# Two-layer streaming encoder: order of work at the entrance of the seven-product feed-forward stage

## The chip, the core and the metric

The kernel runs on one core of a Trainium2 chip. The metric is the device time of one execution in microseconds (us), lower is better. The core's engines run side by side, each through its own queue in order: TensorE (PE in the profile, its weight loads PEld), VectorE (DVE), ScalarE (ACT), GpSimd (POOL), and SyncE (SP), which issues most of the DMA transfers. An engine that waits for a semaphore holds up everything behind it in its own queue.

## The reference, cut to what matters

Two layers. Each projects its input into three mixers, concatenates their outputs, and then does this (`finish` and `conv_ffn` of the reference):

```
x = layer_norm(ALPHA * x + mix @ w_out, ln1_g, ln1_b)
hg = x @ w_gate
hu = x @ w_up
conv = conv_b + sum(conv_w[j] * ext[:, j:j + t] for j in range(3))   # ext: hg with two rows ahead
f = (gelu(conv) * hu) @ w_down
x = layer_norm(ALPHA * x + f, ln2_g, ln2_b)
```

Everything is float32. There are 1024 prompt rows and 128 sample rows, so nine row tiles of 128; D_MODEL is 1024 and D_FF 2816 (22 chunks of 128).

## The kernel before, in words

**Products.** Each float32 operand is split into a high and a low float32r part; a product is three matmuls, high by high, high by low, low by high (`mm3`, L176 to L178). The split is a cast on ScalarE and a subtraction on VectorE. The gate and up projections of one chunk f are not four block products but seven, by a scheme in the manner of Strassen and Winograd: the products A11 by B11, A12 by B21, S2 by T2, S1 by T1, S4 by B22, S3 by T3 and A22 by T4. The A and S operands come from the weights (S1 to S4 are sums of blocks of the chunk's weights), the B and T operands from the normed rows (T1 to T4 are sums of their transposed blocks). The B and T operands are made once a layer; the weight operands anew for each chunk.

**The passage.** It lies between the output projection (`w_out`, product tiles pwo) and the loop over the 22 chunks (product tiles pg), once in each layer: at about 636 to 700 us of the span in layer 0 and 2068 to 2132 us in layer 1. Row tiles 0 to 4 (G1) are already turned into operands ahead of it. Row tiles 5 to 8 (G2, x_5 to x_8 in the rows) go through it one by one. `norm1` calls `norm_rows` on a tile: statistics on VectorE (BN_STATS, BN_AGGR), the small steps to scale and bias (bnsc: plus EPS on VectorE, L211; power of minus one half on GpSimd, L212; minus mean times scale on VectorE, L231), and the norm's application to 128x1024 on ScalarE (L232). Then `pair(j)` follows: eight transposes of the tile on TensorE (L1236), four 512-wide products that bring back B11 and B21 of the partner tile (L1276), eight affine steps on ScalarE (L1290), then on VectorE the sums T1 (L1292), T3 (L1295), T2 (L1296) and T4 (L1298), each split by `put` (L1226, L1227) into the operands: arb holds T1, ara B22, art T2, ar T3 and T4. Pairs 5, 6, 7 and 8 follow each other; pairs 5 to 7 stand among the last `w_out` units and pair 8 after the first two products of chunk 0 (A11 and A12). Then come A11 and A12 of chunk 1 (`early`), then the loop.

**Buffers.** The sum T1 of a pair lies in tail, one buffer for all pairs; tail also holds the weight sum S1. The other sums of a pair lie in temp or in the tile of the pair before. The four product buffers (pg, two PSUM banks each) also serve the transposes of pair 8.

**Weights.** `wnext` makes the next weight operand in a fixed list: A11 and A12 of chunks 0 and 1, then S2, S1, S4, S3 and A22 of chunk 0, and so on. At S2 it makes the sums on GpSimd (L1358 to L1360), at S4 one more (L1362); the split is a cast on ScalarE (L1364) and a subtraction on VectorE (L1365) into one of eight ring slots. Raw weights come by SyncE DMAs into two raw buffers (L1341); a load waits until the last reader of its buffer is through.

**Order.** The program is written in one order, and the build's scheduler then places the instructions on each engine as it thinks best; on an engine they then run strictly in that placed order. `tc.issue_after(i)` keeps what is written under it behind instruction i in the placed order. In the kernel before, T3 and T4 of all four pairs are written after pair 8 (the list `rests`), but the scheduler has put most of them right behind the sums that they split.

## Time and profile before

| what | value |
|---|---|
| median of 3 runs | 2881.7 us (2879.95 to 2882.68) |
| profiled execution, its own time | 2882.72 us |
| its span, first to last instruction | 2880.9 us |
| TensorE busy | 2793.0 us, 97% of the span |
| VectorE, ScalarE, GpSimd busy | 72%, 48%, 31% of the span |
| mean granted TensorE clock | 0.988 of full |

A row of a timeline has start, duration, engine, line, operation, output and inputs, and in brackets how long the engine stood idle before it and what ended that wait. Start-to-start distance is what an instruction costs its engine when the next one waits for nothing; the durations overlap a little. The waits view sums such idle times. The clock column is the granted TensorE clock as a share of 2.4 GHz; 0.5 would be 1.2 GHz throughout. Durations come from the one profiled execution.

### The profile page before, as it was taken

Reading aid. Unit: us, or ns where it says so; the run is one execution under the profiler, and the core shown is the slowest. Engines: PE = TensorE matmul, PEld = TensorE weight load, DVE = VectorE, ACT = ScalarE, POOL = GpSimd, SP = SyncE. Lnnn points to the kernel's source line nnn. Section 1 sums busy time; section 2 is a strip of 40 time slices with the busy share of each in tenths; the row PEclk is TensorE's granted clock in tenths of the full one; section 3 lists DMA queues with packets and bytes.
Section 4 is the critical chain, followed back from the end, with each engine's and each line's share of the span. In section 5 each row is a group of like instructions: output and inputs, shape, how many; then the busy total and the mean of one; then the engine's idle time right before and its main releaser. Section 6 shows DMA issues by size and latency. Waiting matters only on the chain. (4 is left out here: it accounts for less than half of the span.)

```text
span 2880.9 us, 51251 instructions
## 1 busy us (share of the span) xinstructions
PE 2793.0 (97%) x19444; PEld 2613.9 (91%) x19444; DVE 2061.6 (72%) x4580; ACT 1387.3 (48%) x2937; POOL 886.3 (31%) x891
## 2 busy tenths in 40 slices
PE   8999999998999999999999999989989999999998
PEld 8898898998999999888898988989889999997886
DVE  6899878768666666556678997787686666665656
ACT  5687656645333333421256885565553333334211
POOL 2334543443322232000433445334432223220003
PEclk9999999999999999999999999999999999999999
DMA  4121123132212222443212111231322121224421
GB/s 138 53 66 50 43 62 102 58 125 92 72 70 76 76 79 96 158 131 127 79 47 81 39 50 47 56 111 47 121 94 77 69 85 70 72 100 155 153 84 66
DMA packets 105013, 243.15 MB, mean 84 GB/s; under 512 B 21671, under 2 KB 42047, under 8 KB 104767
## 3 DMA queue, kind: packets, MB, share of 16 engines
q1 hardware_dynamic: 88014, 198.59, 21.3%
q10 hardware_dynamic: 16752, 41.29, 3.7%
q8 instruction: 153, 2.51, 0.3%
q14 instruction: 94, 0.76, 0.1%
HBM read 185.20 MB, written 54.64 MB: 83 GB/s over the span
## 5 line engine op out<-in xcount | busy, mean ns | idle before, releaser
L176 PE MATMUL pg<-ar,ring 128*128 128x288 f32 x1408 | 417.1, 296 | 10.1 <-ACT s L1449 4.2
L178 PE MATMUL pg<-ar,ring 128*128 128x288 f32 x1408 | 417.2, 296 | 0.0
L177 PE MATMUL pg<-ar,ring 128*128 128x288 f32 x1408 | 416.5, 296 | 0.0
L1364 ACT CAST ring<-raw 128x512 fp32r<-128x512 f32 x264 | 163.3, 622 | 422.8 <-PE pg L177 401.6
L128 POOL TENSOR_TENSOR ring<-raw,ring 128x512 fp32r<-128x512 f32 (+1 forms) x140 | 191.7, 1396 | 317.9 <-ACT ring L127 270.1
L571 ACT ACTIVATE spare<-sc,cand 128x896 bf16<-128x896 f32 (+5 forms) x262 | 244.7, 934 | 67.3 <-DVE cand L598 21.2
L176 PEld LDWEIGHTS pg<-ar,ring 128*128 128x128 f32 x1408 | 266.1, 189 | 11.7 <-ACT s L1449 4.6
L1365 DVE TENSOR_TENSOR ring<-raw,ring 128x512 fp32r<-128x512 f32 x264 | 203.7, 776 | 90.9 <-ACT ring L1364 90.9
L177 PEld LDWEIGHTS pg<-ar,ring 128*128 128x128 f32 x1408 | 266.2, 189 | 0.0
L178 PEld LDWEIGHTS pg<-ar,ring 128*128 128x128 f32 x1408 | 266.0, 189 | 0.0
L1540 DVE TENSOR_TENSOR s<-s,pg 128x576 f32<-128x576 f32 x220 | 164.4, 749 | 50.8 <-PE pg L178 48.3
L1650 DVE TENSOR_TENSOR acc<-acc,pdn 128x512 f32<-128x512 f32 x180 | 121.3, 683 | 89.3 <-PE pdn L178 88.7
L1484 DVE TENSOR_TENSOR hx<-s,pg 128x512 f32<-128x512 f32 x88 | 60.5, 688 | 150.5 <-PE pg L178 150.5
L176 PE MATMUL pwo<-ring,ar 128*128 128x256 f32 x576 | 166.9, 290 | 0.0
L177 PE MATMUL pwo<-ring,ar 128*128 128x256 f32 x576 | 163.8, 284 | 0.0
L178 PE MATMUL pwo<-ring,ar 128*128 128x256 f32 x576 | 163.8, 284 | 0.0
L565 DVE TENSOR_SCALAR_CACHE_REDUCE spare<-sc,cand 128x384 bf16<-128x384 f32 (+4 forms) x208 | 158.5, 762 | 1.9
L176 PE MATMUL pdn<-ring,ar 128*128 128x512 f32 x360 | 140.1, 389 | 0.0
L177 PE MATMUL pdn<-ring,ar 128*128 128x512 f32 x360 | 140.1, 389 | 0.0
L178 PE MATMUL pdn<-ring,ar 128*128 128x512 f32 x360 | 140.1, 389 | 0.0
L1489 ACT ACTIVATE ct<-hx,cwt 128x512 f32<-128x512 f32 x88 | 71.8, 816 | 127.7 <-DVE hx L1484 127.7
L176 PE MATMUL pvg<-ring,ar 128*128 128x256 f32 x432 | 127.8, 296 | 1.4 <-DVE sg L740 1.4
(427 smaller groups left out, 9434.7 us busy)
## 6 DMA issues: line engine op xcount, KB each, us to landing
raw<-w_gu SPq DMA_DIRECT2D x90, 512.0 KB, 3.8
ad<-ct ACTq DMA_DIRECT2D x44, 576.0 KB, 2.8
raw<-w_d SPq DMA_DIRECT2D x44, 512.0 KB, 4.3
raw<-w_s SPq DMA_DIRECT2D x40, 512.0 KB, 3.9
raw<-w_o SPq DMA_DIRECT2D x32, 512.0 KB, 4.0
araw<-ad SPq DMA_DIRECT2D x48, 288.0 KB, 3.0
s<-ad SPq DMA_DIRECT2D x40, 288.0 KB, 3.6
x1d<-x ACTq DMA_DIRECT2D x18, 512.0 KB, 2.6
```

What stands on the lines that cost most here:

```text
L128: eng.tensor_tensor(l[:, t], raw[:, r], h[:, t].bitcast(F32), ALU.subtract)
L176: nc.tensor.matmul(out, lh, rh, start=first, stop=False)
L177: nc.tensor.matmul(out, lh, rl, start=False, stop=False)
L178: nc.tensor.matmul(out, ll, rh, start=False, stop=last)
L565: nc.vector.tensor_scalar(junkv[:, :w], sc[i], cand[q][:, c:c + 1].bitcast(F32), float(kof(i) - w), op0=ALU.is_lt, op1=ALU.add, accum_out= ...
L571: nc.scalar.activation(junka[:, :w], sc[i], AF.Sign, bias=cand[q][:, c:c + 1].bitcast(F32), scale=-1.0, accum_out=dst)
L1364: nc.scalar.copy(h, src)
L1365: V.tensor_tensor(l, src, h.bitcast(F32), ALU.subtract)
L1484: V.tensor_tensor(hp.rearrange("p (c n) -> p c n", c=2), prompt(sv), prompt(b), ALU.add)
L1489: nc.scalar.activation(cf[:, 512 * h:512 * h + 512], hp, AF.Identity, **kw)
L1540: V.tensor_tensor(out, a, b[:, :, :288], ALU.add)
L1650: V.tensor_tensor(acc[j][:, cs], acc[j][:, cs], po, ALU.add)
```

## The change

The kernel after makes four edits, all in the passage.

1. T1 of a pair lies in one of two buffers in turn, `t1s`, both in ct[0]; tail no longer holds it. The norm's 16 affine columns (lnT) and the statistics move from ct[0] into tail's free end. The load of lnT then stands elsewhere in SyncE's queue: that of layer 0 is at the start of the program, and that of layer 1 between the weight loads and the load of the convolution's weights (cwt) in layer 0's passage.
2. The weight sums S1 to S4 of chunk 0 are made on VectorE, and the first three must stand behind a pair's T2 sum (`hold["sum"]`, pair 8's by then). The four `wnext` calls that stood ahead of pair 8 now follow it, kept behind its affine steps.
3. The splits of T3 and T4 of all pairs (`rests`) must stand behind pair 8's affine steps (casts) and behind its T2 split (subtractions).
4. For row tiles 5 to 8 the three small steps of the norm all run on GpSimd: L226 plus EPS, L227 the power, L238 minus mean times scale.

```diff
--- before.py
+++ after.py
@@ -222,13 +222,20 @@
         for c in halves:
             nc.vector.bn_stats(st[:, c, :], r[:, c * 512:(c + 1) * 512])
         nc.vector.bn_aggr(mv, st)
-        rstd_of(sc[:, 0:1], mv[:, 1:2])
+        if len(halves) == 1:
+            nc.gpsimd.tensor_scalar(sc[:, 0:1], mv[:, 1:2], EPS, None, op0=ALU.add)
+            nc.gpsimd.tensor_tensor(sc[:, 0:1], sc[:, 0:1], mhalf[:, 0:1], ALU.pow)
+        else:
+            rstd_of(sc[:, 0:1], mv[:, 1:2])
         return mv, sc
 
     def norm_rows(r, sp, st=None):
 
         mv, sc = row_stats(r, sp, st)
-        nc.vector.scalar_tensor_tensor(sc[:, 1:2], mv[:, 0:1], -1.0, sc[:, 0:1], op0=ALU.mult, op1=ALU.mult)
+        if st is None:
+            nc.vector.scalar_tensor_tensor(sc[:, 1:2], mv[:, 0:1], -1.0, sc[:, 0:1], op0=ALU.mult, op1=ALU.mult)
+        else:
+            nc.gpsimd.tensor_scalar(sc[:, 1:2], mv[:, 0:1], sc[:, 0:1], -1.0, op0=ALU.mult, op1=ALU.mult)
         nc.scalar.activation(r, r, AF.Identity, bias=sc[:, 1:2], scale=sc[:, 0:1])
 
     def affine_rows(r, g, b, engs):
@@ -1143,9 +1150,9 @@
         hx = xp1.tile([P, 1170], F32, name="hx")
         ct = [xp1.tile([P, 1152], F32, name="ct0")]
         s1 = xp1.tile([P, 2, 288], F32, name="s1")
-        lnT = ct[0][:, 1024:1040].rearrange("p (a k) -> p a k", a=2)
+        lnT = tail[:, 512:528].rearrange("p (a k) -> p a k", a=2)
         nc.sync.dma_start(lnT, d["ln1T"][L])
-        bnj = {j: ct[0][:, 1040 + 12 * n:1052 + 12 * n].rearrange("p (c s) -> p c s", c=2) for n, j in enumerate(G2)}
+        bnj = {j: tail[:, 528 + 12 * n:540 + 12 * n].rearrange("p (c s) -> p c s", c=2) for n, j in enumerate(G2)}
         xg1s = ExitStack()
         xpg = pool(f"xpg_{L}", 1, st=xg1s)
         for j in G1:
@@ -1224,7 +1231,7 @@
         def put(at, n, src, eng):
 
             nc.scalar.copy(at(n, 0), src)
-            eng.tensor_tensor(at(n, 1), src, at(n, 0).bitcast(F32), ALU.subtract)
+            return eng.tensor_tensor(at(n, 1), src, at(n, 0).bitcast(F32), ALU.subtract)
 
         def turned_x(src, where):
 
@@ -1277,31 +1284,29 @@
                 out.append(bv)
             return out
 
+        t1s = ct[0][:, 0:512], ct[0][:, 512:1024]
+
         def pair(j, where, rec):
 
 
             va, vb = turned_x(x1s[j], where)
             at = cols_of(j - 5)
-            t1, t2, t3 = (t.rearrange("p (k t) -> p k t", k=4) for t in (tail[:, 0:512], *temps))
+            t1, t2, t3 = (t.rearrange("p (k t) -> p k t", k=4) for t in (t1s[j % 2], *temps))
             temps[:] = x1s[j][:, 0:512], x1s[j][:, 512:1024]
             b11, b21 = whole(at, ("B11", "B21"), rec)
             for k0, t, v in ((0, t3, va), (4, t2, vb)):
                 for k in range(4):
-                    nc.scalar.activation(t[:, k, :], v[:, k, :], AF.Identity, bias=lnT[:, 1, k0 + k:k0 + k + 1],
+                    hold["affine"] = nc.scalar.activation(t[:, k, :], v[:, k, :], AF.Identity, bias=lnT[:, 1, k0 + k:k0 + k + 1],
                                          scale=lnT[:, 0, k0 + k:k0 + k + 1])
             V.tensor_tensor(t1, t3, b11, ALU.subtract)
             put(at, "T1", t1, V)
             put(at, "B22", t2, V)
             V.tensor_tensor(t3, t2, t3, ALU.subtract)
-            V.tensor_tensor(t2, t2, t1, ALU.subtract)
-            put(at, "T2", t2, V)
+            hold["sum"] = V.tensor_tensor(t2, t2, t1, ALU.subtract)
+            hold["split"] = put(at, "T2", t2, V)
             V.tensor_tensor(t2, b21, t2, ALU.subtract)
 
-            def rest():
-                put(at, "T3", t3, V)
-                put(at, "T4", t2, V)
-
-            return rest
+            rests.extend(((at, "T3", t3), (at, "T4", t2)))
 
         def pair_dec():
             at = cols_of(4)
@@ -1354,12 +1359,14 @@
                 raw_load(0, 0)
             a11, a12, a21, a22 = (raws.get((f, c)) for c in range(4))
             src = {"A11": a11, "A12": a12, "S1": tail[:, 0:512], "S2": a11, "S3": a21, "S4": a12, "A22": a22}[n]
+            e = G if f else V
             if n == "S2":
-                G.tensor_tensor(tail[:, 0:512], a21, a22, ALU.add)
-                G.tensor_tensor(a21, a11, a21, ALU.subtract)
-                G.tensor_tensor(a11, tail[:, 0:512], a11, ALU.subtract)
+                with ExitStack() if f else tc.issue_after(hold["sum"].ins):
+                    e.tensor_tensor(tail[:, 0:512], a21, a22, ALU.add)
+                    e.tensor_tensor(a21, a11, a21, ALU.subtract)
+                    e.tensor_tensor(a11, tail[:, 0:512], a11, ALU.subtract)
             if n == "S4":
-                G.tensor_tensor(a12, a12, a11, ALU.subtract)
+                e.tensor_tensor(a12, a12, a11, ALU.subtract)
             h, l = wslot((4 + i) % 8)
             nc.scalar.copy(h, src)
             V.tensor_tensor(l, src, h.bitcast(F32), ALU.subtract)
@@ -1402,8 +1409,8 @@
             if s == 1:
                 V.bn_stats(bnj[j][:, 0, :], x1s[j][:, 0:512])
             if s == 3 and j > 5:
-                rests.append(pair(j - 1, where(), where()))
-            if j == 8 and s >= 2:
+                pair(j - 1, where(), where())
+            if (s, j) == (2, 8):
                 for _ in range(4):
                     wnext()
         pst.close()
@@ -1448,12 +1455,18 @@
         early("A11", 0, "B11")
         nc.scalar.copy(s1, first["A11", 0][:, :, :288])
         early("A12", 0, "B21")
-        rests.append(pair(8, where(), where()))
+        pair(8, where(), where())
+        for _ in range(4):
+            with tc.issue_after(hold["affine"].ins):
+                wnext()
         early("A11", 1, "B11")
         early("A12", 1, "B21")
         rest_dec()
-        for r in rests:
-            r()
+        for at, n, t in rests:
+            with tc.issue_after(hold["affine"].ins):
+                nc.scalar.copy(at(n, 0), t)
+            with tc.issue_after(hold["split"].ins):
+                V.tensor_tensor(at(n, 1), t, at(n, 0).bitcast(F32), ALU.subtract)
         turn1.clear()
         for _ in range(wnext.late):
             wnext()
```

Where the instructions stand now, in layer 0. Layer 1 has these sequences too, with other buffer numbers and a DMA issue or an affine step a place or two earlier; line numbers of the changed kernel are its own.

GpSimd, from the last split of the sample rows' T2 (art from x4d) to the small steps of the later tiles. Before:

```order
L1227 TENSOR_TENSOR art<-x4d,art 128x8x32
L212 TENSOR_TENSOR bnsc<-bnsc,mhalf 128x1
L1264 TENSOR_TENSOR x4d<-ar,x4d 128x256
L1227 TENSOR_TENSOR ar<-x12d,ar 128x8x32
L1265 TENSOR_TENSOR x4d<-x4d,ar 128x256
L212 TENSOR_TENSOR bnsc<-bnsc,mhalf 128x1 x2
L1227 TENSOR_TENSOR ar<-x4d,ar 128x8x32
```

After:

```order
L1234 TENSOR_TENSOR art<-x4d,art 128x8x32
L226 TENSOR_SCALAR bnsc<-bnmv 128x1
L1271 TENSOR_TENSOR x4d<-ar,x4d 128x256
L227 TENSOR_TENSOR bnsc<-bnsc,mhalf 128x1
L1234 TENSOR_TENSOR ar<-x12d,ar 128x8x32
L1272 TENSOR_TENSOR x4d<-x4d,ar 128x256
L238 TENSOR_SCALAR bnsc<-bnmv,bnsc 128x1
L226 TENSOR_SCALAR bnsc<-bnmv 128x1
L227 TENSOR_TENSOR bnsc<-bnsc,mhalf 128x1
L238 TENSOR_SCALAR bnsc<-bnmv,bnsc 128x1
```

A tile's norm had one instruction here; it has three. The first tile's three are interleaved with three operations of the sample rows (x4d, x12d), which are `pair_dec` and `rest_dec`.

ScalarE, from the first cast of a weight sum or the first affine step of pair 8 (x_7 is written) on. Before:

```order
L1364 CAST ring<-tail 128x512
L1226 CAST ar<-x_6_8057 128x4x128
L1364 CAST ring<-raw 128x512 x4
L1449 COPY s_6481<-pg 128x576
L1489 ACTIVATE ct_6480<-hx,cwt 128x512
L1290 ACTIVATE x_7_8059<-trx,ct_6480 128x128 x8
L1226 CAST arb<-tail 128x4x128
L1226 CAST ara<-x_7_8059 128x4x128
L1490 ACTIVATE ct_6480<-hx,cwt 128x64
L1226 CAST ar<-x_7_8059 128x4x128
L1226 CAST art<-x_7_8059 128x4x128
L1364 CAST ring<-tail 128x512
```

After:

```order
L1371 CAST ring<-raw 128x512
L1456 COPY s_6481<-pg 128x576
L1299 ACTIVATE x_7_8059<-trx,tail 128x128 x8
L1467 CAST ar<-temp_8456 128x4x128
L1467 CAST ar<-temp_8455 128x4x128
L1467 CAST ar<-x_5_8055 128x4x128 x2
L1467 CAST ar<-x_6_8057 128x4x128 x2
L1233 CAST arb<-ct_6480 128x4x128
L1233 CAST ara<-x_7_8059 128x4x128
L1467 CAST ar<-x_7_8059 128x4x128
L1233 CAST art<-x_7_8059 128x4x128
L1371 CAST ring<-tail 128x512
```

The copy of the first product (s from pg) and pair 8's affine steps moved ahead of the casts of the weight sums (ring from tail and raw); six casts of T3 and T4 (L1467, of the pairs 5 to 7) now stand between pair 8's affine steps and its T1 cast (arb from ct).

VectorE, from pair 8's second operand (ara; its T1 split arb stands just ahead) to the add of the product S2 (s from s and pg, L1540 before, L1553 after). Before:

```order
L1227 TENSOR_TENSOR ara<-x_7_8059,ara 128x4x128
L1227 TENSOR_TENSOR ar<-x_7_8059,ar 128x4x128
L1296 TENSOR_TENSOR x_7_8059<-x_7_8059,tail 128x512
L1227 TENSOR_TENSOR art<-x_7_8059,art 128x4x128
L1298 TENSOR_TENSOR x_7_8059<-trx,x_7_8059 128x512
L1365 TENSOR_TENSOR ring<-tail,ring 128x512
L1227 TENSOR_TENSOR ar<-x_7_8059,ar 128x4x128
L1540 TENSOR_TENSOR s_6481<-s_6481,pg 128x576
L1365 TENSOR_TENSOR ring<-raw,ring 128x512 x3
```

After, in two pieces that follow each other:

```order
L1234 TENSOR_TENSOR ara<-x_7_8059,ara 128x4x128
L1305 TENSOR_TENSOR x_7_8059<-x_7_8059,ct_6480 128x512
L1365 TENSOR_TENSOR tail<-raw 128x512
L1366 TENSOR_TENSOR raw<-raw 128x512
L1234 TENSOR_TENSOR art<-x_7_8059,art 128x4x128
L1469 TENSOR_TENSOR ar<-temp_8456,ar 128x4x128
L1469 TENSOR_TENSOR ar<-temp_8455,ar 128x4x128
L1469 TENSOR_TENSOR ar<-x_5_8055,ar 128x4x128 x2
L1469 TENSOR_TENSOR ar<-x_6_8057,ar 128x4x128 x2
L1469 TENSOR_TENSOR ar<-x_7_8059,ar 128x4x128
L1372 TENSOR_TENSOR ring<-tail,ring 128x512
```

```order
L1367 TENSOR_TENSOR raw<-tail,raw 128x512
L1307 TENSOR_TENSOR x_7_8059<-trx,x_7_8059 128x512
L1372 TENSOR_TENSOR ring<-raw,ring 128x512
L1369 TENSOR_TENSOR raw<-raw 128x512
L1372 TENSOR_TENSOR ring<-raw,ring 128x512
L1469 TENSOR_TENSOR ar<-x_7_8059,ar 128x4x128
L1372 TENSOR_TENSOR ring<-raw,ring 128x512
L1372 TENSOR_TENSOR ring<-tail,ring 128x512
L1553 TENSOR_TENSOR s_6481<-s_6481,pg 128x576
```

Seven of the eight T3 and T4 subtractions (L1469) and three of the four sums of chunk 0 (L1365 to L1367; the fourth is L1369) stand here now. S2's own sum is L1367, raw from tail and raw. The low part of chunk 1's S1 (ring from tail, the row ahead of L1553) stands ahead of the add now, as it did before.

## Rows read from the trace of the kernel before

**Rows 1.** The page's busy times: engine, busy us, share of the span, instructions

```profile
PE 2793.0 (97%) x19444; PEld 2613.9 (91%) x19444; DVE 2061.6 (72%) x4580; ACT 1387.3 (48%) x2937; POOL 886.3 (31%) x891
```

**Rows 2.** Windows of 10 us, layer 0: busy by engine (count), PEclk, DMA

```profile
670.00:680.00 10.00, 6.66 (x32) 6.67 (x33) 7.15 (x11) 7.67 (x17) 1.58 (x1) 0.66 0.33 107
680.00:690.00 10.00, 10.00 (x77) 10.00 (x77) 9.28 (x12) 4.40 (x8) 6.18 (x4) 1.00 0.00 0
```

**Rows 3.** TensorE's waits, layer 0, 636 to 720: total us, times, longest

```profile
PE pg L176 <- ACT s L1449: 4.2, 1, 4.2
PE trx L1236 <- ACT x L232: 3.1, 2, 1.7
PE trx L1276 <- DVE x L1298: 1.4, 1, 1.4
PE pg L176 <- DVE s L1540: 0.7, 1, 0.7
PE pg L176 <- ACT x L1290: 0.2, 1, 0.2
```

**Rows 4.** TensorE's waits, layer 1, 2068 to 2150

```profile
PE pg L176 <- DVE x L1298: 4.1, 1, 4.1
...
PE pg L176 <- ACT x L1290: 1.6, 1, 1.6
PE pg L176 <- DVE s L1540: 1.1, 1, 1.1
```

**Rows 5.** Timeline of VectorE, layer 0: the small steps, then sums and splits

```profile
636.91 0.15 DVE L211 TENSOR_SCALAR bnsc<-bnmv 128x1 f32<-128x1 f32 x1
...
661.73 0.68 DVE L1227 TENSOR_TENSOR arb<-tail,arb 128x512 fp32r<-128x512 f32 x1
662.33 0.68 DVE L1298 TENSOR_TENSOR x<-trx,x 128x512 f32<-128x512 f32 x1
...
665.50 1.60 DVE L1227 TENSOR_TENSOR art<-x,art 128x512 fp32r<-128x512 f32 x1
...
668.70 1.76 DVE L1227 TENSOR_TENSOR ar<-x,ar 128x512 fp32r<-128x512 f32 x1
```

**Rows 6.** Timeline of GpSimd, layer 0

```profile
637.15 0.55 POOL L212 TENSOR_TENSOR bnsc<-bnsc,mhalf 128x1 f32<-128x1 f32 x1 [0.20 <-DVE bnsc L211]
637.66 0.74 POOL L1264 TENSOR_TENSOR x4d<-ar,x4d 128x256 f32<-128x256 f32 x1
638.36 0.72 POOL L1227 TENSOR_TENSOR ar<-x12d,ar 128x256 fp32r<-128x256 f32 x1
```

**Rows 7.** Timeline of ScalarE, layer 0: norm applied, two casts, affine steps

```profile
638.46 1.24 ACT L232 ACTIVATE x<-x,bnsc 128x1024 f32<-128x1024 f32 x1 [2.32 <-DVE bnsc L231]
...
654.41 0.65 ACT L1226 CAST ar<-temp 128x512 fp32r<-128x512 f32 x1
654.93 0.65 ACT L1226 CAST ar<-x 128x512 fp32r<-128x512 f32 x1
...
675.28 2.88 ACT L1290 ACTIVATE x<-trx,ct 128x128 f32<-128x128 f32 x8
```

**Rows 8.** Small steps on GpSimd: the power, all 36 (min/median/max ns)

```profile
L212 POOL TENSOR_TENSOR bnsc<-bnsc,mhalf x36: 540/551/1397, 575.6 to 2875.2; 128x1 f32<-128x1 f32 x36
```

**Rows 9.** GpSimd's groups: a small copy (busy us, mean ns, idle before)

```profile
L1499 POOL COPY tails<-hx 128x16 f32<-128x16 f32 x44 | 8.5, 194 | 0.0
```

**Rows 10.** Timeline of TensorE, layer 0: pair 8's four 512-wide products

```profile
667.95 1.19 PE L1276 MATMUL trx<-ar,identr 128*128 128x512 f32 x4 [1.42 <-DVE x L1298]
```

**Rows 11.** Raw weights, 600 to 720: GpSimd's sum (ns), DMA to landing

```profile
L1358 POOL TENSOR_TENSOR tail<-raw x4: 1292/1400/1600, 664.9 to 719.5; 128x512 f32<-128x512 f32 x4
...
DMA to landing us min/median/max: 3.7/3.9/5.4
```

**Rows 12.** The page's costliest groups: the add of a product

```profile
L1540 DVE TENSOR_TENSOR s<-s,pg 128x576 f32<-128x576 f32 x220 | 164.4, 749 | 50.8 <-PE pg L178 48.3
```

## The prediction

> **What bounds the kernel now.** I read the page's busy times first: TensorE is busy 2793.0 of 2880.9 us [rows 1], so only what makes it wait, or runs it at the lower clock, can move the time. The diff touches the passage alone, so the second view is TensorE's waits there, by who ended them [rows 3, 4]. The reader is to see that they are few: in layer 0 4.2 us behind ScalarE's copy of the first product (L1449), 3.1 us in two waits (so 1.4 and 1.7) behind the application of the norm (L232), 1.4 us behind VectorE's T4 sum (L1298), 0.7 us behind the first add (L1540), and 0.2; in layer 1 4.1, 3.1 in a row that reads the same as layer 0's, 1.6 and 1.1. The third view is the windows: from 670 to 680 us the granted clock is 0.66, so part of the window ran at 1.2 GHz; its 32 matmuls took 6.66 us, where the next window, at 2.4 GHz, has 77 in 10 us, 0.13 us each [rows 2]. At 0.13 the 32 would take 4.2 us; the low clock cost 2.4 us, after the 4.2 us wait. I take 2.4 for layer 1 too, whose wait is as long. All waits and this loss make 12.0 us in layer 0 and 12.3 in layer 1: no change of this kind can give back more than some 24 us, 0.8%.
>
> What can take their place is read from the timelines, by walking each engine's queue in its new order with the durations that its instructions had. The distances that I use: on VectorE a 128x512 sum or split starts 0.60 us after the one before it and lasts 0.68 (661.73, 662.33) [rows 5]; on ScalarE a cast takes 0.52 from start to start and lasts 0.65, pair 8's eight affine steps 2.9 [rows 7]; on GpSimd an operation of the sample rows takes 0.70 from start to start, the power 0.51 and lasts 0.55 [rows 6]; the adding of a product takes 0.75 [rows 12].
>
> **The norm's small steps on GpSimd (first transposes).** Before, BN_AGGR of the first tile is done at 636.9; VectorE adds EPS, GpSimd's power starts at 637.15, VectorE multiplies, and ScalarE applies the norm at 638.46 [rows 5 to 7]. Two operations of VectorE with 0.15 us go, and two with [128x1] come to GpSimd. Its queue now reads: L226, a sample-row operation, L227, two more, L238. Where before the sample rows' three stood behind the power, all three are now between BN_AGGR and ScalarE. No row shows such a step on GpSimd. The nearest from above is the longest of the powers, 1.40 us [rows 8]; from below a small copy, 0.19 [rows 9]. I take the power's usual 0.55, the nearest in shape (0.5 start to start). Then: 637.0 + 0.5 + 0.7 + 0.5 + 2 x 0.7 + 0.55 = 640.65 against 638.46. **+2.2 us** at the first transposes, in both layers, as the norm's application is what TensorE waits for there. With 0.19 it is +1.5, with 1.40 +3.9. A gain is excluded: even free steps leave three sample-row operations of 0.7 in a chain that had none. Tiles 6 to 8 have no sample-row work in between and gain or lose under 1 us each, which I put into the range.
>
> **Pair 7 and the first product.** In ScalarE's new order the norm of x_7 stands ahead of four casts that it stood behind; the wait of 1.7 before pair 7's transposes goes: **-1.7** in both layers. But four casts (4 x 0.52 = 2.1) now lie between that norm and pair 7's affine steps, and the first product's buffer is free only after those. I take the wait there (0.2 and 1.6 before) as 2.2 after: **+2.0** in layer 0, **+0.6** in layer 1.
>
> **Pair 8 and the products of chunk 1.** The copy L1449 no longer stands behind casts that wait for GpSimd's sums, and T1's second buffer takes the wait of 1.4 behind T4's sum away. So 1.4, 4.2 and the low clock's 2.4 go in layer 0, 4.1 and 2.4 in layer 1: **-8.0** and **-6.5**.
>
> **S2 by T2: what is late next.** Let T be the start of pair 8's affine steps on ScalarE. TensorE then finishes the 512-wide products (1.19 us in all, the last 0.8 behind T) [rows 10] and 48 matmuls of A11 and A12 of chunk 1 (6.2): it is free at T + 7.0. S2's weights come by a chain that the new order makes long:
> - ScalarE: eight affine steps 2.9, six casts of T3 and T4 at 0.52 = 3.1, T1's cast 0.65: T + 6.65.
> - VectorE's T1 split waits for that cast, and everything is behind it. Up to L1367, which makes S2, stand 14 pieces (T1 and B22 split, T2's sum, two weight sums, T2's split, seven T3 and T4 splits, S1's low part) at 0.60 = 8.4, then L1367 itself, 0.68: T + 15.75.
> - ScalarE casts S2, 0.65: T + 16.4.
>
> So TensorE waits 16.4 - 7.0 = **+9.4 us** ahead of S2, in both layers. It waited for nothing there before: the T3 and T4 splits of the earlier pairs were spread over the 20 us ahead, in gaps of both engines, and GpSimd made the sums. The sums' own 3 x 0.60 are the small part; the seven splits (4.2) and the six casts (3.1) are the large one. The load of cwt also moves, behind the split of the temp buffers, but lands about when S2's sum is done; nothing for it.
>
> Here the trace shows one thing in favour: beside GpSimd's sums VectorE's splits took 1.60 and 1.76 instead of 0.68 [rows 5]. The Trainium skill says why, on the page SBUF — State Buffer, section "Who interferes with whom": a VectorE instruction with two SBUF inputs and a GpSimd one that reads SBUF share one port, and one of them blocks. The trace agrees with 1.76 against 0.68. By that rule the moved sums free VectorE; what this would give is the first rival below.
>
> **S4 by B22: the second new wait.** With S2's start as S, its product and S1's keep TensorE until S + 6.2. S4's buffer is freed by the add of S2's product, L1553. Ahead of that on VectorE stands the low part of chunk 1's S1, which needs chunk 1's raw weights, whose load waits for the last split of chunk 0's S4. From L1367 at S - 1.75 that split begins six pieces (3.6) later and ends at S + 2.5; DMA 3.9, GpSimd's sum 1.4 [rows 11]; ScalarE's cast 0.65, the low part 0.68, the add 0.75: S + 9.9. TensorE waits 3.7, and the 0.7 and 1.1 of before go: **+3.0** and **+2.6**. The DMA took 3.7 to 5.4, so 3.5 to 5.2 of waiting.
>
> **The clock after.** A wait of 9.4 us will bring 1.2 GHz again; the first one did after 4.2. Where it falls I can't tell. Inside the wait it costs nothing; all of S2 and S1 at half speed cost 6.2, of which S4's wait of 3.7 takes most: 0 to 2.5 a layer, taken as **+0.5**.
>
> **Sum.** Layer 0: 2.2 - 1.7 + 2.0 - 8.0 + 9.4 + 3.0 + 0.5 = 7.4. Layer 1: 2.2 - 1.7 + 0.6 - 6.5 + 9.4 + 2.6 + 0.5 = 7.1. Together 14.5 us. The profiled execution took 2882.7 us for its span of 2880.9; 2897.2 then, and with the median 1.0 lower, 2881.7, **2896 us**, +0.5%.
>
> **Rivals.**
> - *VectorE is relieved and the change does what it says* (not slower). If the freed port decides, VectorE gets through its pieces sooner: the waits and the low clock of pair 8 go (-8.0 and -6.5), no new wait comes at S2 or S4 (-0.7, -1.1 too), and only the first +2.2 and pair 7 (+0.3, -1.1) remain: -12.7, 2869 us. For it: the stretched rows of 1.60 and 1.76. Against it: S2's wait is already worked out with the short 0.68 throughout. It would need 9.4 us less than 14 such pieces and the casts ahead of them take, which is more than all 14 (8.4). It decides only if the splits and S2's sum ran in another order than the one placed.
> - *Both unknown prices at their low end.* Small steps of 0.19 (-0.7 a layer) and chunk 1's raw weights in time, so no wait at S4 (-3.7 a layer), no clock loss (-0.5): 4.9 a layer less, +4.7 in all, 2886 us: no change that can be told. Against it: the load waits for a split that is itself late.
> - *The small steps are dear.* At 1.40 the first wait is +1.7 more, and the norm of x_7, three steps in a chain that had one, comes some 2 us later and brings pair 7's wait back: +3.7 a layer, 2904 us. For it: the longest power took 1.40. Against it: the median is 0.55.
>
> **Chances.** My forecast 0.62, small steps dear 0.14, low end 0.14, relieved 0.10. The forecast's own bounds (first wait 1.5 to 3.9, DMA 3.7 to 5.4, clock 0 to 2.5) give 2892 to 2902. The range 2885 to 2905 takes in the low end and the dear steps and leaves the relieved case out. A measurement of this kernel tells about 0.2%, 5.8 us: below 2876 is faster, above 2887.5 slower. Faster 0.10, the same 0.14, slower 0.76.
>
> **What would show it.** In the profile after: TensorE's waits in the passage led by one of about 9 us ahead of the first S2 product (pg from art), ended by ScalarE's cast L1371, in each layer; the second by VectorE's add L1553, about 3.5 us; the first transposes waiting 3.6 us instead of 1.4; no wait of 4 us behind the copy of the first product. VectorE without a gap of note from the T1 split of pair 8 to L1367, about 8.4 us. I am wrong if S2's wait is under 4 us, or if the small steps of the norm, L226 and L238, show under 0.2 us and the first transposes wait no longer than before.

## The result, and the profile after

The changed kernel takes 2903.5 us, the median of four runs (2900.7 to 2905.5), where four runs of the kernel before, on the same chip, took 2882.2 (2880.0 to 2883.3). The medians differ by 21.3 us; the ratio on record is 1.0070, with a 95% interval of 1.0058 to 1.0082, some 20 us slower. I had said 2896 us and a range of 2885 to 2905.

The profiled execution took 2900.7 us for a span of 2899.0. Its busy times, beside [rows 1]:

```profile
PE 2796.0 (96%) x19444; PEld 2618.2 (90%) x19444; DVE 2058.2 (71%) x4572; ACT 1388.7 (48%) x2937; POOL 880.1 (30%) x899
```

No engine has more work: the time is in TensorE's waits and in its clock. TensorE's waits in layer 0, 636 to 720 us, beside [rows 3]:

```profile
PE pg L176 <- ACT ring L1371: 9.4, 1, 9.4
PE pg L176 <- DVE s L1553: 3.3, 1, 3.3
PE trx L1243 <- ACT x L239: 3.3, 1, 3.3
PE pg L176 <- ACT x L1299: 1.6, 1, 1.6
```

In layer 1, 2068 to 2160 us, beside [rows 4], the first and the third of these read alike, and the other two are:

```profile
PE pg L176 <- DVE s L1553: 2.3, 1, 2.3
PE pg L176 <- DVE ct L1301: 2.1, 1, 2.1
```

The waits of 4.2, 1.4 and 4.1 us are gone, and so is the 1.7 ahead of pair 7. A wait of 9.4 us has come, ended by the cast L1371 that makes S2's weights, and one of 3.3 or 2.3 behind the add L1553. The three instructions at which TensorE waits longest in layer 0 (start, duration, last the wait):

```profile
641.09 1.97 PE L1243 MATMUL trx<-identr,x 128*128 128x128 f32 x8 [3.26 <-ACT x L239]
...
685.51 0.61 PE L176 MATMUL pg<-art,ring 128*128 128x288 f32 x1 [9.39 <-ACT ring L1371]
...
696.79 0.58 PE L176 MATMUL pg<-ara,ring 128*128 128x288 f32 x1 [3.30 <-DVE s L1553]
```

Each of the three is followed by work at the lower clock. The windows of layer 0, beside [rows 2] (PEclk is the third column from the right):

```profile
640.00:650.00 10.00, 8.91 (x59) 8.57 (x60) 4.99 (x8) 6.72 (x13) 0.92 (x3) 0.83 0.26 105
670.00:680.00 10.00, 6.12 (x47) 5.88 (x45) 5.88 (x10) 8.28 (x18) 0.00 (x0) 0.92 0.01 1
680.00:690.00 10.00, 4.49 (x23) 4.49 (x24) 8.41 (x14) 2.99 (x5) 1.32 (x1) 0.57 0.29 86
690.00:700.00 10.00, 6.70 (x40) 6.50 (x39) 5.22 (x6) 3.10 (x5) 5.75 (x4) 0.77 0.11 41
700.00:710.00 10.00, 10.00 (x70) 10.00 (x69) 8.20 (x12) 2.94 (x5) 3.07 (x4) 0.89 0.36 107
710.00:720.00 10.00, 10.00 (x77) 10.00 (x76) 8.98 (x15) 5.86 (x8) 3.77 (x4) 1.00 0.16 62
```

Before, the clock was low in one stretch of the passage; now it is in three, at 641, at 678 to 688 and at 695 to 702 us. In layer 1 it is in four: one more stands behind the wait of 2.1 us. The eight transposes at 641 take 1.97 us where they took 1.1.

Why S2's weights are late is read from VectorE, layer 0:

```profile
675.43 0.69 DVE L1234 TENSOR_TENSOR arb<-ct,arb 128x512 fp32r<-128x512 f32 x1 [2.94 <-ACT arb L1233]
...
679.30 1.29 DVE L1469 TENSOR_TENSOR ar<-temp,ar 128x512 fp32r<-128x512 f32 x2
680.51 3.09 DVE L1469 TENSOR_TENSOR ar<-x,ar 128x512 fp32r<-128x512 f32 x5
683.52 0.69 DVE L1372 TENSOR_TENSOR ring<-tail,ring 128x512 fp32r<-128x512 f32 x1
684.12 0.68 DVE L1367 TENSOR_TENSOR raw<-tail,raw 128x512 f32<-128x512 f32 x1
```

and from ScalarE:

```profile
668.86 2.91 ACT L1299 ACTIVATE x<-trx,tail 128x128 f32<-128x128 f32 x8 [1.06 <-PE trx L1243]
671.62 1.18 ACT L1467 CAST ar<-temp 128x512 fp32r<-128x512 f32 x2
672.65 2.23 ACT L1467 CAST ar<-x 128x512 fp32r<-128x512 f32 x4
674.74 0.66 ACT L1233 CAST arb<-ct 128x512 fp32r<-128x512 f32 x1
...
684.84 0.62 ACT L1371 CAST ring<-raw 128x512 fp32r<-128x512 f32 x1 [1.04 <-DVE raw L1367]
```

Read them in turns. VectorE stands still for 2.94 us for T1's cast, because six casts of T3 and T4 went ahead of it on ScalarE. Then VectorE works without a gap from 675.43 to 684.80, seven splits of T3 and T4 (4.2 us) in the middle, and only then is S2's sum (L1367) there to cast.

S4's wait is read from VectorE too. The add of S2's product (L1553), which frees S4's buffer, stands behind the low part of chunk 1's S1 (ring from tail), and that waits for chunk 1's raw weights:

```profile
694.78 1.21 DVE L1372 TENSOR_TENSOR ring<-tail,ring 128x512 fp32r<-128x512 f32 x1 [6.36 <-ACT ring L1371]
695.91 0.74 DVE L1553 TENSOR_TENSOR s<-s,pg 128x576 f32<-128x576 f32 x1
```

**Where the 20 us are.** TensorE runs the same 19444 matmuls in both traces, so I subtract the starts of the same matmul, less the difference at the start of the passage:

| after minus before, us | behind the first transposes | S2's start | S4's start | end of passage |
|---|---|---|---|---|
| layer 0 measured | 3.3 | 3.8 | 8.7 | 10.3 |
| layer 0 forecast | 2.2 | 3.9 | 6.9 | 7.4 |
| layer 1 measured | 3.4 | 6.5 | 11.2 | 11.5 |
| layer 1 forecast | 2.2 | 4.0 | 6.6 | 7.1 |

The passages lose 21.8 us in this trace; the rest of the program differs by -3.8. The same code outside the passages differs by -3.8 to +3.9 us between the profiled executions below, so I compare passages from traces and whole times from the medians.

### The profile page after: what moved, and what is told of

It reads as the page before. It is cut to its first block, busy times and chain, and to the rows that moved or that the text cites. A ratio compares the mean times of both kernels' runs of the same rounds, so it can differ in the third digit from the quotient of the medians.

```text
span 2899.0 us, 51255 instructions
## 1 busy us (share of the span) xinstructions
PE 2796.0 (96%) x19444; PEld 2618.2 (90%) x19444; DVE 2058.2 (71%) x4572; ACT 1388.7 (48%) x2937; POOL 880.1 (30%) x899
## 3 DMA queue, kind: packets, MB, share of 16 engines
q1 hardware_dynamic: 88014, 198.59, 21.3%
## 5 line engine op out<-in xcount | busy, mean ns | idle before, releaser
L1371 ACT CAST ring<-raw 128x512 fp32r<-128x512 f32 x264 | 163.8, 622 | 436.3 <-PE pg L177 396.4
L1372 DVE TENSOR_TENSOR ring<-raw,ring 128x512 fp32r<-128x512 f32 x264 | 207.6, 788 | 89.9 <-ACT ring L1371 89.9
L1553 DVE TENSOR_TENSOR s<-s,pg 128x576 f32<-128x576 f32 x220 | 164.5, 749 | 49.0 <-PE pg L178 46.7
```

Of the source, the lines that this page charges most:

```text
L1371: nc.scalar.copy(h, src)
L1372: V.tensor_tensor(l, src, h.bitcast(F32), ALU.subtract)
L1553: V.tensor_tensor(out, a, b[:, :, :288], ALU.add)
```

## The experiments

Theory: the order of VectorE's and ScalarE's queues makes S2's wait (the held T3 and T4 pieces), and the waits bring the low clock. Rival 1: the weight sums on VectorE. Rival 2: the norm's small steps and the clock behind them. All times are medians; the column in us is the ratio to the kernel before, run on the same chip, times 2882. "Passages" is what both passages of the profiled execution lose against the kernel before, as in the table above.

| kernel | ratio (95%) | us over before | passages, layer 0 and 1 |
|---|---|---|---|
| changed kernel | 1.0070 (1.0058 to 1.0082) | +20 | +10.3, +11.5 |
| e1 no hold | 1.0031 (1.0019 to 1.0042) | +9 | +4.9, +8.1 |
| e2 norm back | 1.0039 (1.0026 to 1.0051) | +11 | +7.4, +5.9 |
| e3 sums on GpSimd | 1.0065 (1.0053 to 1.0077) | +19 | +9.6, +12.5 |
| e4 T3, T4 behind S4 | 1.0029 (1.0017 to 1.0041) | +8 | +4.7, +6.3 |
| e5 no hold, norm back | 1.0022 (1.0012 to 1.0032) | +6 | -0.5, +5.9 |
| e6 waits filled | 1.0056 (1.0042 to 1.0071) | +16 | +8.1, +8.7 |
| e7 two T1 alone | 1.0031 (1.0019 to 1.0043) | +9 | +4.3, +4.8 |
| e8 e5 and sums back | 1.0035 (1.0022 to 1.0048) | +10 | +2.6, +5.7 |
| e9 two T1, sums on VectorE | 1.0018 (1.0009 to 1.0026) | +5 | +3.3, +3.3 |
| e10 norm alone | 1.0032 (1.0020 to 1.0043) | +9 | +2.6, +3.9 |
| e11 e4 and norm back | 1.0013 (1.0004 to 1.0021) | +4 | +2.7, +2.1 |
| e12 before, wait filled | 1.0001 (0.9992 to 1.0010) | 0 | +0.5, 0.0 |

### What makes S2's wait: e1, e4, e3

e1, T3 and T4 where each pair makes them:

```diff
         for at, n, t in rests:
-            with tc.issue_after(hold["affine"].ins):
-                nc.scalar.copy(at(n, 0), t)
-            with tc.issue_after(hold["split"].ins):
-                V.tensor_tensor(at(n, 1), t, at(n, 0).bitcast(F32), ALU.subtract)
+            put(at, n, t, V)
```

> The T3 and T4 casts and splits are issued again where each pair makes them, not behind pair 8; all else as in the changed kernel. Theory (queue order): seven splits and six casts that stand ahead of S2's sum on VectorE and ScalarE make the wait of 9.4 us ahead of the first S2 product. Ahead of L1367 there now stand some seven pieces of VectorE at 0.60 us behind T1's cast instead of 14, so the wait falls to 2 to 3 us in each layer, the long stretch of low clock behind it goes with it, and the time to 2884 to 2890 us. Rival 1 (the three weight sums on VectorE themselves make the wait): it stays above 7 us and the time above 2897. Rival 2 (the norm's small steps and the clock that falls after them carry most): the time stays above 2895, with the first wait at 3.3 us.

Measured: 2892.9 us. TensorE's longest waits in layer 0:

```profile
PE trx L1243 <- ACT x L239: 3.2, 1, 3.2
PE pg L176 <- DVE s L1550: 2.8, 2, 1.9
PE pg L176 <- ACT ring L1371: 2.7, 1, 2.7
```

S2's wait fell to 2.7 us, 2.2 in layer 1, as the theory said, with the sums still on VectorE: rival 1 falls as the main cause, but for the rest of 2.7, which goes when the sums are on GpSimd again (e8). The time came 3 us above the theory's range: in layer 1 the first product now waits 3.8 us behind a T1 sum, and S4 4.2. In layer 0 S4 waits only 0.9: there the add of S2's product stands ahead of chunk 1's low part on VectorE, in layer 1 behind it.

e4, their splits behind chunk 0's S4 split:

```diff
-            with tc.issue_after(hold["affine"].ins):
+            with tc.issue_after(hold["S4"].ins):
                 nc.scalar.copy(at(n, 0), t)
-            with tc.issue_after(hold["split"].ins):
                 V.tensor_tensor(at(n, 1), t, at(n, 0).bitcast(F32), ALU.subtract)
```

(`hold["S4"]` is the split L1372 of that piece.)

> The splits of T3 and T4 are issued behind chunk 0's S4 split instead of behind T2's split; the sums stay on VectorE, the small steps on GpSimd. Theory (queue order): seven pieces fewer ahead of L1367, S2's wait falls from 9.4 to about 2 us in each layer; the wait of S4 by chunk 1's low part stays near 3 us; the low clock falls to what follows the first transposes and S4. Time 2884 to 2890. Rival 1 (the sums): S2's wait stays above 7 us, time above 2897. Rival 2 (the small steps): above 2895.

Measured: 2893.6 us. TensorE's longest waits in layer 0:

```profile
PE pg L176 <- DVE s L1552: 4.9, 1, 4.9
...
PE pg L176 <- ACT ring L1371: 2.1, 1, 2.1
```

S2's wait is 2.1 us in both layers, as worked out; the time is 4 us above the range. The miss is S4's wait: 4.9, and 5.3 in layer 1, instead of 3. The moved splits do not make it, though they stand ahead of chunk 1's low part, for VectorE has done them and stands idle there (the splits end at 688.57):

```profile
691.11 0.87 DVE L1372 TENSOR_TENSOR ring<-tail,ring 128x512 fp32r<-128x512 f32 x1 [2.54 <-ACT ring L1371]
```

S4 starts 11.5 and 11.9 us behind S2, where the changed kernel has 11.3 in both layers. What differs is TensorE: with the granted clock at 1.00 it is through S2 and S1 in 6.6 us instead of 8.0 and 9.0, and waits the longer for the same chain.

e3, the sums on GpSimd again:

```diff
-            e = G if f else V
+            e = G
```

> All weight sums on GpSimd as in the kernel before; T3 and T4 still bunched, small steps still on GpSimd. In the order S2's cast and split then stand ahead of the bunch and T2's split behind it. Theory (queue order): the wait ahead of the first S2 product is now for T2 (art) and not for the weights: eight affine steps 2.9, four weight casts 2.1, six casts 3.1, T1's cast 0.65, then T1, B22, T2's sum and split on VectorE, some 11.2 us after the affine steps start against 7.0 of TensorE's work: a wait of 4 to 5 us instead of 9.4, and S4's wait under 1.5 us, since chunk 1's weights are asked for earlier. Time 2882 to 2890. Rival 1 (the sums' own time on VectorE, 1.8 us a layer): 2898 to 2901. Rival 2 (the small steps): above 2898.

Measured: 2903.3 us, nothing gained: the theory's 2882 to 2890 is missed, and the time alone is what rival 2 asked for (above 2898), but the rows show a new wait. S2's weights were early, as expected; the next product, S1 by T1, waits 8.0 us in layer 0 (5.7 in layer 1) behind the T4 sum L1307, for the bank that it frees. VectorE, layer 0, ahead of that sum:

```profile
683.71 3.45 DVE L1469 TENSOR_TENSOR ar<-temp,ar 128x512 fp32r<-128x512 f32 x2
687.08 5.23 DVE L1469 TENSOR_TENSOR ar<-x,ar 128x512 fp32r<-128x512 f32 x5
```

The seven held splits now run beside GpSimd's sums of chunk 1 and take 8.6 us instead of 4.3. So taking the sums off GpSimd does relieve VectorE, as the prediction's first rival claimed; but what is relieved is the held splits, which the change itself put there. That rival is wrong about the change and right about the mechanism.

### The norm's small steps: e2, e10

e2 takes the norm's edits out of the changed kernel, e10 puts them alone into the kernel before:

```diff
+        if len(halves) == 1:
+            nc.gpsimd.tensor_scalar(sc[:, 0:1], mv[:, 1:2], EPS, None, op0=ALU.add)
...
+            nc.gpsimd.tensor_scalar(sc[:, 1:2], mv[:, 0:1], sc[:, 0:1], -1.0, op0=ALU.mult, op1=ALU.mult)
```

> The norm's small steps are made as in the kernel before (VectorE adds EPS and multiplies, GpSimd takes the power); all else as in the changed kernel. Theory (queue order): the wait ahead of the first transposes falls from 3.3 to 1.4 us and the half-clock stretch at these transposes goes, together about 3 us a layer; the wait of 9.4 us ahead of S2 stays. Time 2896 to 2899. Rival 2 (the small steps carry most, through the clock): under 2892. Rival 1 (the sums): 2897 to 2900, not told from the theory here.

> The kernel before with the norm's small steps on GpSimd alone. Theory: the first transposes wait 3.3 us instead of 1.4 in each layer and run at half clock (1.0 to 1.6 us), and nothing later takes it up: 6 to 7 us in all, 2887 to 2890 us. Rival (a later wait in the passage takes it up, since ScalarE and VectorE get ahead meanwhile): 2881 to 2885 us. Rival (the low clock spreads further, as the 9 us that the changed kernel gained by undoing this part would have it): 2890 to 2894 us.

Measured: 2896.4 and 2892.5 us. In e2 the first transposes wait 1.4 us again, S2 9.4 still; the passages gain 2.9 and 5.5 us. In e10 they lose 2.6 and 3.9, 6.5 together, the theory's size; the median's 9 us (2892.5) is above it, in the range of the second rival, and its interval (6 to 12 us) holds both. The 3 us between I leave open. GpSimd in the changed kernel, beside [rows 6]:

```profile
636.55 0.25 POOL L226 TENSOR_SCALAR bnsc<-bnmv 128x1 f32<-128x1 f32 x1
...
637.46 0.57 POOL L227 TENSOR_TENSOR bnsc<-bnsc,mhalf 128x1 f32<-128x1 f32 x1
...
639.50 0.27 POOL L238 TENSOR_SCALAR bnsc<-bnmv,bnsc 128x1 f32<-128x1 f32 x1
```

The steps are cheap; what costs is that the sample rows' three operations, 0.7 each, stand between them. Rival 2 holds for some 7 to 9 of the 20 us, not for most.

### What the low clock costs: e6, e12

e6 keeps TensorE at work in the two new waits:

```diff
             xo, b = opx[x], banks("pg")
+            for i in range({"S2": 64, "S1": 24}.get(n, 0) if f == 0 else 0):
+                xf = opx["B21"][:, 0, i % 4, :]
+                nc.tensor.matmul(b[:, 0, :288], xf[:, 0:128], xf[:, 0:288], start=True, stop=True)
```

> The changed kernel with TensorE kept at work in its two new waits of each layer: 64 matmuls of 128x288 ahead of chunk 0's S2 product (8.3 us at 0.13) and 24 ahead of its S1 product (3.1 us), written into the product's own buffer and overwritten by it; they read B21 alone. The chains on VectorE, ScalarE and GpSimd are as in the changed kernel, so S2 and S4 cannot start earlier than there. Theory (the clock that falls after these waits is the term that I sized at 0.5 us a layer and that costs some 3): no half-clock stretch behind S2's and S4's start, 2 to 3.5 us less a layer, 2896 to 2900 us beside 2903.5 of the changed kernel. Rival (the waits alone make the loss, the clock nothing): 2902 to 2905 us.

Measured: 2897.5 us. The intervals of e6 and of the changed kernel overlap, so the times do not decide. Windows of e6 in layer 0:

```profile
680.00:690.00 10.00, 9.09 (x69) 8.86 (x69) 10.00 (x17) 4.22 (x8) 1.32 (x1) 1.00 0.20 50
690.00:700.00 10.00, 10.00 (x77) 10.00 (x77) 3.92 (x5) 2.34 (x4) 4.74 (x4) 1.00 0.24 79
700.00:710.00 10.00, 8.59 (x63) 8.15 (x62) 8.89 (x13) 3.61 (x7) 3.87 (x5) 1.00 0.31 107
```

The granted clock, 0.57, 0.77 and 0.89 in the changed kernel, is 1.00 throughout, and the passages are 2.2 and 2.8 us shorter. But that is not the clock's price, since two other things changed with it. The filler held S2 back:

```profile
677.86 8.59 PE L1432 MATMUL pg<-ar 128*128 128x288 f32 x64
687.36 2.63 PE L1432 MATMUL pg<-ar 128*128 128x288 f32 x18 [0.91 <-DVE x L1307]
689.83 0.29 PE L176 MATMUL pg<-art,ring 128*128 128x288 f32 x1
```

S2 begins 12.1 us behind the last matmul of A12 (677.73), where the changed kernel needed 9.7; 2.4 us of filler too much. And the build placed VectorE's instructions in another order, against what I had expected: the add of S2's product now stands ahead of chunk 1's low part, in both layers:

```profile
694.80 0.76 DVE L1556 TENSOR_TENSOR s<-s,pg 128x576 f32<-128x576 f32 x1 [4.49 <-PE pg L178]
697.01 1.23 DVE L1372 TENSOR_TENSOR ring<-tail,ring 128x512 fp32r<-128x512 f32 x1 [1.45 <-ACT ring L1371]
```

So S4 no longer waits for chunk 1's raw weights, whatever the clock: it begins 7.2 us behind S2 instead of 11.3. From S4's start to chunk 1's S2 e6 takes 11.4 and 11.3 us, waits of 1.4 and 1.3 in it, where the changed kernel took 12.1 and 11.1 without a wait. In layer 1, besides, the low clock behind the first product (1.5 us) stayed away, where no filler stands. e6 shows that the filler keeps the clock; what the clock costs behind S2 and S4 it does not show. It shows something else, as e1's two layers do: with the add ahead of chunk 1's low part the second wait is short or gone. No run changes that order alone.

e12 does the same to the kernel before, whose one long wait had brought the clock down too [rows 2]:

```diff
+        def fill(b):
+            for i in range(32):
+                xf = opx["B11"][:, 0, i % 4, :]
+                nc.tensor.matmul(b[:, 0, 288:512], xf[:, 0:128], xf[:, 0:224], start=True, stop=True)
...
+        if not L:
+            fill(first["A12", 0])
         early("A11", 1, "B11")
```

> The kernel before, with TensorE kept at work in its one long wait of each passage: 32 matmuls of 128x224 (some 3.3 us) into columns 288 to 511 of a product's bank, which nothing reads; in layer 0 between pair 8's transposes and chunk 1's first product, in layer 1 between chunk 0's first and second product. No chain of the other engines is changed. Theory (the low clock behind a wait is a cost of its own): the half-clock stretch of 6.8 us behind these waits goes, 2.4 us a layer, and the time falls to 2876 to 2880 us, under both kernels. Rival (what the clock gives is taken back by the next wait, since VectorE sets the pace of the passage): 2880.5 to 2884 us.

Measured: 2881.3 us, and 2881.0 for the kernel before: no gain. Windows and TensorE of e12, layer 0:

```profile
670.00:680.00 10.00, 9.31 (x75) 9.13 (x74) 8.49 (x13) 7.61 (x17) 1.89 (x2) 1.00 0.31 106
```

```profile
669.32 3.73 PE L1451 MATMUL pg<-ar 128*128 128x224 f32 x32
673.73 0.40 PE L176 MATMUL pg<-ar,ring 128*128 128x288 f32 x1 [0.69 <-ACT s L1456]
682.37 0.40 PE L177 MATMUL pg<-art,ring 128*128 128x288 f32 x1 [0.30 <-DVE art L1227]
688.97 0.40 PE L176 MATMUL pg<-ara,ring 128*128 128x288 f32 x1 [1.67 <-DVE s L1549]
699.75 0.37 PE L176 MATMUL pg<-art,ring 128*128 128x288 f32 x1 [0.97 <-DVE s L1549]
```

The clock stayed at 1.00 and the 2.4 us were won, and then waited for: 0.30 at T2's split, 1.67 at S4, where there was no wait before, and 0.97 instead of 0.67 at chunk 1's S2. The rival holds here: VectorE's order in the passage is that of the kernel before, and the low clock is not paid where a later wait follows whose end does not hang on the slowed matmuls. The changed kernel beside e4 says the same of the low clock behind S2: S4 does not start sooner without it. Where the later work hangs on the slowed matmuls, as behind the first transposes, it is paid: without that wait and its clock (3.3 us, e2) S2 starts 3.1 us earlier in layer 0.

### The other parts, and whether a version gains: e5, e7, e8, e9, e11

e5 is e1 with the norm back, e11 is e4 with the norm back, e8 is e5 with e3's line. e7 and e9 go from the kernel before:

```diff
-            t1, t2, t3 = (t.rearrange("p (k t) -> p k t", k=4) for t in (tail[:, 0:512], *temps))
+            t1, t2, t3 = (t.rearrange("p (k t) -> p k t", k=4) for t in (t1s[j % 2], *temps))
```

with `lnT`, `bnj` and `t1s` as in the change; e9 also takes chunk 0's sums to VectorE where they stand (`e = G if f else V`).

> Both the T3/T4 hold and the norm's small steps undone; two T1 buffers and chunk 0's sums on VectorE behind pair 8's sum stay. Theory (queue order, and the clock with the waits): what the two undone parts gave apart adds up, 12 us without the hold and 9 us without the small steps against the changed kernel's 21 us of loss; time 2882 to 2886 us, first wait 1.4 us, S2's wait 2 to 3 us. Rival (the parts share one loss, the low clock, so that the second brings little): 2888 to 2891 us.

> The kernel before with the first edit alone (two buffers for T1). Theory: the waits behind T4's sum that freed T1's single buffer go (1.4 us in layer 0, 4.1 in layer 1), but S1's cast now comes ahead of pair 6's and pair 7's casts on ScalarE and waits there for GpSimd's sums, so that up to 3 us a layer may come back before the first product's copy: 2876 to 2883 us. Rival (the buffer was not what TensorE waited for): 2881 to 2884 us with both waits as before. Rival (the earlier cast holds ScalarE up more than the buffer gives): above 2885 us.

> The changed kernel without the hold, with the norm's steps and all sums as before: two T1 buffers stay, and the four weight pieces of chunk 0 issued behind pair 8. Theory (queue order): the first product's copy no longer stands behind casts that wait for GpSimd (4.2 us less in layer 0, and the low clock's 2.4), S2's weights are made by GpSimd in time; T2's split comes some 2 us later by the four casts ahead of T1's, a wait of 0 to 2 us. 2872 to 2880 us. Rival (VectorE beside GpSimd's sums, with splits of 1.6 to 1.8 us, is late again): 2881 to 2888 us.

> The kernel before with two T1 buffers and chunk 0's weight sums on VectorE in their old place (not held behind pair 8's sum); norm and T3/T4 as before. With two T1 buffers alone the wait behind T4's sum had grown to 4.9 us in layer 0 and 8.5 in layer 1, beside splits of 1.6 to 1.8 us next to GpSimd's sums. Theory (VectorE's queue is full there, 0.60 us a piece without a gap): four sums add 2.4 us, two or three stretched splits give back 1.0 each, so the wait behind T4's sum stays at 4 to 5 and 7 to 8.5 us; 2886 to 2891 us. Rival (the sums on GpSimd beside VectorE are the trouble, and moving them is the gain that the change was after): that wait falls under 2 us, 2876 to 2882 us.

> T3's and T4's splits behind chunk 0's S4 split, and the norm's small steps as before; two T1 buffers and the sums on VectorE stay. Theory (the parts add): the version with these splits behind S4 lost 8 us, and the small steps were worth 6 to 9 of the changed kernel's loss: 2882 to 2887 us, S2's wait about 2 us, S4's about 5, first transposes 1.4. Rival (VectorE's queue is the bound, and what is gained ahead is waited for at S4): 2887 to 2891 us.

Measured: e5 2888.9, e7 2890.6, e8 2891.7, e9 2887.8, e11 2886.4 us. e5 missed the theory's 2882 to 2886: the two parts do not add up, which fits its rival. e11 fits the theory: S2's wait 2.6, and 3.9 in layer 0 behind the adds of products (1.1 at S4, the rest at chunk 1's S2). e8 missed by more than 10 us, and its rival's range by 4: with GpSimd's sums back, TensorE waits 3.7 and 7.8 us behind VectorE's T4 sum. e7's time is that of its third reading (above 2885), but TensorE waits for VectorE there, not for ScalarE's cast; its first waits in layers 0 and 1, and e9's below:

```profile
PE trx L1276 <- DVE x L1300: 4.9, 1, 4.9
...
PE pg L176 <- DVE x L1300: 8.5, 1, 8.5
```

```profile
PE trx L1276 <- DVE x L1300: 4.5, 1, 4.5
...
PE pg L176 <- DVE x L1300: 7.4, 1, 7.4
```

The second buffer frees S1's weight pieces to go earlier, and there they stand ahead of the T4 sum that frees a pair's bank: 1.4 and 4.1 us of waiting [rows 3, 4] became 4.9 and 8.5. With the sums on VectorE it is 4.5 and 7.4: moving them is worth 0.4 and 1.1 us at this wait, since VectorE has no gap there and takes them at 0.60 each. None of the versions beats the kernel before; e12 alone equals it.

## Why the prediction was right, and which term was off

The direction, the main wait and the range were right; 2896 was 7.5 us short. 2903.5 lies above the bounds that I gave the forecast itself, 2892 to 2902; these do not add up, since every term at its end gives 2893 to 2907. The range reached to 2905 for a rival that did not come true, so that it held the time is in part luck. By its steps:

- **First transposes, +2.2.** The wait is 3.3 us, +1.84, in both layers; forecast 3.6. The first tile's steps took 0.25, 0.57 and 0.27, where I took 0.55 for each. But +3.3 and +3.4 were lost: behind this wait the clock fell as well, 1.5 us that the sum did not have.
- **Pair 7, -1.7.** It went, and e2 shows that the order did it, since it stays away with the norm's steps back.
- **First product, +2.0 and +0.6.** It waits 1.6 and 2.1 us (2.2 forecast). In layer 1 the passage lost 1.95 there, 1.3 more than forecast, 1.5 of it in the product's own matmuls behind the wait, with the granted clock at 0.84 in the window.
- **Pair 8 and chunk 1's products, -8.0 and -6.5.** Between the same matmuls -8.6 in layer 0, -6.5 in layer 1. e12 adds that the clock's 2.4 in it was no gain by itself: in the kernel before it would have been waited for later.
- **S2, +9.4.** 9.4 us in both layers, ended by L1371, with VectorE gapless for 9.4 us from T1's split to the end of L1367 (9.1 forecast); e1 and e4 show that the held pieces are the cause. This step held in every part.
- **S4, +3.0 and +2.6.** The wait is 3.3 and 2.3 us (3.7 forecast), and the 0.7 of before that I counted off stood three products later, at chunk 1's S2; it went all the same. S4 starts 11.3 us behind S2 in both layers, where I had 9.9: the chain to the add was 1.4 longer. From S2's start to S4's 4.9 and 4.7 us were lost, against the 3.7: the wait, and 1.6 and 2.4 us by which the two products were slower at the lower clock. The chain alone sets the sum of the two: at full clock the wait would have been longer by as much, as in e4.
- **The clock after, +0.5.** This is the term that was off. I priced the low clock once, behind S2, and there it went as I had it: S4's wait took up what the two products lost. What I left at nothing is the low clock behind the other waits. It cost 1.5 us a layer at the first transposes, 1.5 at layer 1's first product, and 2.5 and 1.6 behind S4's start, where matmuls stand 0.24 us apart instead of 0.13 (the passage pays 1.7 and 0.3 of these, for the 0.7 and 1.1 at chunk 1's S2, counted off above, go with them). That is 4.0 us in layer 0 and 4.6 in layer 1, 7.6 more than my 0.5 a layer. The whole miss of the passages is 7.3 (21.8 against 14.5), for two other misses cancel: S4's chain was 2.2 dearer than forecast, and the steps up to S2's start, without the clock, 2.2 cheaper. These prices are read from rows and from starts of the same matmuls; no run takes the clock away alone.

Of the rivals, "relieved" fell with S2's wait. "Low end" fell with S4's wait and the clock, though the small steps came near its 0.19. "Small steps dear" came nearest in its time, 2904, by the wrong cause: the steps were cheaper than I took them. On the stretched splits, the Trainium skill's page SBUF — State Buffer, section "Who interferes with whom", says that a VectorE instruction with two SBUF inputs contends with a GpSimd instruction that reads SBUF. The rows of e3 agree (8.6 us for seven splits beside GpSimd's sums against 4.3).

## What to carry to other kernels

An edit that lets an instruction go later is to be read by what it queues up with: pieces that filled gaps for nothing cost their full time once they stand in a row ahead of one that TensorE waits for. Price a new wait together with the lower clock that may follow it, each wait for itself, and ask whether a later wait takes the loss back: one whose end does not hang on the slowed matmuls does. An experiment that adds instructions can change the order in which the build places the others; compare the queues before a difference is put down to what was added. And where VectorE has no gap, taking over a small sum or freeing a buffer early moves the wait and does not remove it.

## What I had not expected of the hardware

- Behind the wait of 3.3 us eight transposes took 1.97 us, and the granted clock of the window was 0.83. Behind the 1.4 at the same place in e2 they took 1.09, at 1.00.
- Matmuls whose results nobody reads kept the granted clock at 1.00 behind the filled waits (e6, e12), and in e12, where VectorE's order in the passage is unchanged, that gave nothing.
- Behind the same wait of 2.1 us at layer 1's first product the clock fell in the changed kernel (0.84 in the window) and stayed at 1.00 in e6.
- GpSimd's [128x1] steps took 0.25 and 0.27 us for the first tile, half of the power's 0.57; for the last tile, beside VectorE's sums and splits, 0.65, 0.86 and 0.81.
- Splits of 0.60 us on VectorE took 1.0 to 1.7 on average beside GpSimd's 128x512 sums (e3), seven in a row.
